# A decoder layer on one core: the first norm's steps put ahead of modulation rows and weight remainders, and a longer skew in the last down pass

## The chip, the cores and the metric

The kernel runs on one core of a Trainium2 chip. The time is what the device takes for one execution, in microseconds; the kernel before was run three times, and the median is 1267.68 us (1267.37 to 1270.29). Another execution was profiled, and the rows below are from it. The engines of the core are TensorE (PE: matmuls and transposes; PEld is its weight load), VectorE (DVE), ScalarE (ACT), GpSimd (POOL) and SyncE (SP), which here issues all transfers.

## The reference

The kernel computes one layer of a decoder over 256 tokens of width 2048, in float32. A conditioning vector gives six modulation vectors (shift, scale, gate for each of two sub-layers). The first sub-layer mixes tokens in two groups of heads and ends with an output projection; the second is a gated feed-forward network of inner width 5632. After each, a layer norm:

```python
mod = c_act @ w_mod[l] + b_mod[l]
sh1, sc1, g1, sh2, sc2, g2 = jnp.split(mod[:, None, :], N_MOD, axis=-1)
u = x * (1.0 + sc1) + sh1
y = token_mixer(u, w_in[l], conv_w[l], conv_b[l], b_igate[l], b_fgate[l],
                mlstm_norm_w[l], hgrn_norm_w[l], lb_all[l], w_out[l])
x = layer_norm(DEEPNORM_ALPHA * x + (1.0 + g1) * y, ln1_g[l], ln1_b[l])
u = x * (1.0 + sc2) + sh2
y = swiglu(u, w_gate[l], w_up[l], w_down[l])
x = layer_norm(DEEPNORM_ALPHA * x + (1.0 + g2) * y, ln2_g[l], ln2_b[l])
```

## The kernel before

**Weights in two parts.** Every float32 weight tile (128 x 1024, 512 KB) is loaded by SyncE into a buffer of `wr` (four of them), ScalarE copies it to the rounded type that TensorE takes (`wh`, five buffers), and VectorE subtracts that copy from the original: the remainder `wl` (five buffers). Activations are split likewise. A product is then three matmuls (`three`, L710 to L717): high x high (L713), low x high (L714), high x remainder (L717). `w1` (L699) makes one such tile.

**Modulation rows.** `mod(j)` (L171 to L174) loads one block of 128 rows of the modulation weight (1 MB) into one of two buffers of `mr` and reduces it on VectorE against the conditioning vector into a column of `modc`. There are 96: 32 at the start, 34 drawn by `mods_some` through the mixer and the output projection (`modq`), 14 named `late`, two of which `some(2)` issues for each k from 2 on in the first feed-forward groups, and 16 later. From these columns `affine1(c)` makes scale and shift for a quarter c of the normalised activations (`sc`, lines 786 to 788). The quarters 2 and 3 take them from `late` rows, quarter 3 from the last of them.

**Output projection** (L750 to L775). Two parts, four column groups c, four weight tiles each; the 256 tokens are two halves t, each with a PSUM bank. In the last group all four tiles are taken for half 0 and then for half 1. After each group `resid` scales the bank by the gate and adds it to z (L724, L728), and `stat` gathers the norm's statistics (L731).

**First norm.** `norm1(t)` aggregates (L735), takes logarithm and exponential on ScalarE, and scales z in four pieces (L802). `turn` transposes z on TensorE (L809, 16 transposes for a half) and `make_u2` applies scale and shift on ScalarE and splits the result into `u2h` and `u2l` (L830). A quarter c of u2 is used by the feed-forward blocks k = 4c to 4c + 3.

**Feed-forward.** The first two inner groups run together (`ffn_in((0, 1))`): 16 blocks k, each with two weight tiles and 24 matmuls, using all eight PSUM banks. k = 0 and 1 are done for half 0, then half 1 is transposed, then they are done for half 1. Nine more groups follow one by one, in two stretches, each with a pass of the down projection behind it (`down`); SiLU (`swi`) takes the banks at the end of a group. `fix` and `affine` (L914, L915) prepare z for the second residual on VectorE.

**The end.** The last down pass takes inner blocks 24 to 43, ten weight tiles for each of four column groups. In the last group the last `skew` = 8 blocks (four tiles) are done for half 0, then for half 1. Then `resid`, `stat` and `finish(t)`: the norm, two VectorE steps for each of four pieces (L970, L971), and the store.

**Order.** Each engine works through its instructions in an order fixed when the program is built. A planner lists the instructions as they become ready in its own estimate of time and takes the one earliest in the program first; `tc.high_priority(n)` lets instructions count as n places earlier in the program, and `add_manual_dep` with this kind of dependency sets only an order. Weight copies and remainders have n = 400.

Of the kernel before, what the change touches and what calls it, by code (L numbers as in the profile page):

```python
# [3 lines left out]
F32 = mybir.dt.float32  # L4
F32R = mybir.dt.float32r
U8 = mybir.dt.uint8
AF = mybir.ActivationFunctionType
ALU = mybir.AluOpType

P = 128  # L10
# [5 lines left out]
ALPHA = 2.0 ** 0.25  # L16
# [21 lines left out]
FIRST = 34  # L38
MIX = (("qk g i", "first"), ("v", "second"), ("o", "p last n"))
NATIVE = ((), ())  # L40
PRI = dict(w=400, e=0, m=-200)

PK = {}
_at = 0
# [10 lines left out]
RATE = (0.45, 0.4, 0.5)  # L55
# [24 lines left out]
def build(nc, tc, d):  # L80
    from contextlib import ExitStack

    with ExitStack() as ctx:
        cst = ctx.enter_context(tc.tile_pool(name="cst", bufs=1))
        wr = ctx.enter_context(tc.tile_pool(name="wr", bufs=CFG["wr"]))
        wh = ctx.enter_context(tc.tile_pool(name="wh", bufs=CFG["wh"]))
        wl = ctx.enter_context(tc.tile_pool(name="wl", bufs=CFG["wl"]))
# [6 lines left out]
        cnt = [0]  # L94
# [5 lines left out]
        def M(n=1024, name="m", dt=F32):  # L100
            cnt[0] += 1
            return med.tile([P, n], dt, tag="m", name=f"{name}{cnt[0]}")
# [11 lines left out]
        table = {"set": None, "load": None, "used": []}  # L114
# [19 lines left out]
        tt = nc.vector.tensor_tensor  # L134
# [36 lines left out]
        def mod(j):  # L171
            t = mr.tile([P, D], F32, tag="m", name=f"m{j}")
            nc.sync.dma_start(t, d["wmod"][j])
            table["mod"] = nc.vector.tensor_tensor_reduce(t, t, cb, 1.0, init[:, j : j + 1], ALU.mult, ALU.add, modc[:, j : j + 1]).ins  # L174
            yield

        def run(gen):
            for _ in gen:
                pass
# [440 lines left out]
        def mods_some(a):  # L620
            credit[0] += a
            while credit[0] >= 1:
                credit[0] -= 1
                next(modq, 0)
# [38 lines left out]
        for names, gen, n in PLAN:  # L663
# [4 lines left out]
            c = 0.0  # L668
# [27 lines left out]
                act(o[:, 512 * c : 512 * c + 512], bank, AF.Copy)  # L696
            return o

        def w1(src):  # L699
            cnt[0] += 1  # L700
            r = wr.tile([P, 1024], F32, tag="w", name=f"wr{cnt[0]}")
            nc.sync.dma_start(r, src)
            h = wh.tile([P, 1024], F32R, tag="h", name=f"wh{cnt[0]}")
            l = wl.tile([P, 1024], F32R, tag="l", name=f"wl{cnt[0]}")
            with tc.high_priority(PRI["w"]):
                act(h, r, AF.Copy)
                tt(l, r, h.bitcast(F32), ALU.subtract)  # L707
            return h, l

        def three(banks, h, l, a, b, first, last):  # L710
# [10 lines left out]
        def resid(t, c, bank, gate, scale):  # L721
            w = slice(512 * c, 512 * c + 512)
            m = S(512, "s5", bufs=CFG["s5"])
            tt(m, bank, gate[:, w], ALU.mult)  # L724
            if scale is None:
                tt(z[t][:, w], z[t][:, w], m, ALU.add)
            else:
                stt(z[t][:, w], z[t][:, w], scale, m, ALU.mult, ALU.add)  # L728

        def stat(t, c):  # L730
            nc.vector.bn_stats(st[t][:, 6 * c : 6 * c + 6], z[t][:, 512 * c : 512 * c + 512])  # L731
# [18 lines left out]
        for part in (1, 0):  # L750
            for c in range(4):
                if part:
                    banks[c] = [ps(), ps()]
                tiles = []
                skew = part == 0 and c == 3
                for p in range(4):
                    tiles.append(w1(d["wo"][16 * (1 - part) + 4 * c + p]))
                    mods_some(RATE[2])
                    if not skew:
                        for t in range(2):  # L760
                            for j in range(2):
                                k = 8 * part + 2 * p + j
                                w = slice(512 * j, 512 * j + 512)
                                three([banks[c][t]], tiles[-1][0][:, w], tiles[-1][1][:, w], half(yh, k, t), half(yl, k, t), part == 1 and k == 8, part == 0 and k == 7)
                if skew:
                    for t in range(2):
                        for p in range(4):
                            for j in range(2):
                                k = 2 * p + j
                                w = slice(512 * j, 512 * j + 512)  # L770
                                three([banks[c][t]], tiles[p][0][:, w], tiles[p][1][:, w], half(yh, k, t), half(yl, k, t), False, k == 7)
                if part == 0:
                    for t in range(2):
                        resid(t, c, banks[c][t], G1, ALPHA)
                        stat(t, c)  # L775
        run(modq)
        late = order2[FIRST:]

        def some(n):
            for _ in range(n):  # L780
                if late:
                    run(mod(late.pop(0)))

        def affine1(c):
            w = slice(4 * c, 4 * c + 4)
            tt(Ac[:, w], pc("l1g", 4 * c, 4), modc[:, 64 + 4 * c : 68 + 4 * c], ALU.mult)
            tt(Bc[:, w], pc("l1b", 4 * c, 4), modc[:, 64 + 4 * c : 68 + 4 * c], ALU.mult)
            tt(Bc[:, w], Bc[:, w], modc[:, 48 + 4 * c : 52 + 4 * c], ALU.add)

        affine1(0)  # L790
        affine1(1)
        u2h = [M(name="u2h", dt=F32R) for _ in range(4)]
        u2l = [M(name="u2l", dt=F32R) for _ in range(4)]

# [3 lines left out]
        def norm1(t):  # L798
            mu, rs = norm(t)
            for c in range(4):  # L800
                w = slice(512 * c, 512 * c + 512)
                ts(z[t][:, w], z[t][:, w], mu, rs, ALU.subtract, ALU.mult)  # L802

        zt = {}

        def turn(t, c):
            bank = ps()
            for j in range(4):
                nc.tensor.transpose(bank[:, P * j : P * j + P], z[t][:, 512 * c + P * j : 512 * c + P * j + P], ident)  # L809
            if c < 2:  # L810
                zt[t, c] = bank
                return
            if t == 0:
                zt[c] = M(name="zt")
            zt[t, c] = zt[c][:, 512 * t : 512 * t + 512]
            act(zt[t, c], bank, AF.Copy)

        def make_u2(t, c):
            u = S(512, "s5", bufs=CFG["s5"])
            for j in range(4):  # L820
                k = 4 * c + j
                w = slice(P * j, P * j + P)
                act(u[:, w], zt[t, c][:, w], AF.Identity, scale=Ac[:, k : k + 1], bias=Bc[:, k : k + 1])

            def part(x):
                return x[c].rearrange("p (k t) -> p k t", t=T)[:, :, t * P : t * P + P]

            u3 = u.rearrange("p (k t) -> p k t", t=P)
            act(part(u2h), u3, AF.Copy)
            tt(part(u2l), u3, part(u2h).bitcast(F32), ALU.subtract)  # L830
# [40 lines left out]

            return bk, held, block

        norm1(0)
        for c in range(4):
            turn(0, c)
            if c < 2:
                make_u2(0, c)
        norm1(1)
        use_set(AF.Silu)  # L880
        tc.add_manual_dep(table["load"], table["var"].name, order, reason="table")
        bk, held, block = ffn_in((0, 1))
        for k in range(2):
            for g in range(2):
                held[k, g] = w1(d["wf"][g * KT + k])
            block(k, 0)
        for c in range(4):
            turn(1, c)
            if c < 2:
                make_u2(1, c)  # L890
        for k in range(2):
            block(k, 1)
        for k in range(2, KT):
# [44 lines left out]
        def down(k0, k1, G, last):  # L938
            for c in range(4):
                bk = [ps(), ps()]  # L940
                held = {}
                skew = 8 if last and c == 3 else 0

                def pair(k, t):
                    for j in range(2):
                        w = slice(512 * j, 512 * j + 512)
                        three([bk[t]], held[k][0][:, w], held[k][1][:, w], hslice(k + j, t, 0), hslice(k + j, t, 1), k + j == k0, k + j == k1 - 1)

                for k in range(k0, k1, 2):
                    held[k] = w1(d["wd"][22 * c + k // 2])  # L950
                    if k < k1 - skew:
                        for t in range(2):
                            pair(k, t)
                    if k == k0 + 4:
                        while pend:
                            flip(pend.pop(0))
                for t in range(2):
                    for k in range(k1 - skew, k1, 2):
                        pair(k, t)
                    resid(t, c, bk[t], G, None)  # L960
                    if last:
                        stat(t, c)
                        if c == 3:
                            finish(t)

        def finish(t):
            mu, rs = norm(t)
            for c in range(4):
                w = slice(512 * c, 512 * c + 512)
                stt(z[t][:, w], z[t][:, w], mu, Lg[:, w], ALU.subtract, ALU.mult)  # L970
                stt(z[t][:, w], z[t][:, w], rs, Lb[:, w], ALU.mult, ALU.add)  # L971
                nc.sync.dma_start(d["out"][t][:, w], z[t][:, w])
# [73 lines left out]
```

## Time and profile before

| | |
|---|---|
| three runs | 1267.37, 1267.68, 1270.29 us |
| profiled execution | 1270.38 us, its span 1268.6 us |
| TensorE busy | 1216.6 us, 96% |
| VectorE busy | 900.4 us, 71% |
| ScalarE busy | 588.6 us, 46% |
| moved by DMA | 328 MB, 259 GB/s in the mean |

The span is the time from the first instruction to the last. An engine's line gives its busy time and share of the span. The chain that ended last is followed back from the last instruction to whatever released it, step by step. In rows in order of time the first number is the start and the second the time to the end of the last instruction in the row; the bracket at the end is how long the engine had been idle and what released it. Matmuls overlap: each lasts 0.39 us, and they start 0.2265 us apart at full clock.

### The profile page before, as it was taken

What the parts mean: (1) busy time and instruction counts of PE and PEld (TensorE: products, weight loads), DVE (VectorE), ACT (ScalarE), POOL (GpSimd) and SP (SyncE); (2) the same over time, 40 slices, a digit from 0 to 9 for tenths busy, and PEclk for the clock granted to TensorE, in tenths of its full rate; (3) what the DMA queues carried; (4) which work ended last, traced back from release to release, by engine and by line L of the source; (5) the groups of instructions that cost most, each with busy time, mean ns of one, the idle gap of its engine ahead of it and who ended that gap; (6) DMA issues with size and microseconds to landing.
All of it is one profiled execution on the core that took longest, in us unless ns stands there. A gap on an engine that the chain in (4) does not pass through costs nothing.

```text
span 1268.6 us, 17191 instructions
## 1 busy us (share of the span) xinstructions
PE 1216.6 (96%) x6738; PEld 1045.5 (82%) x6738; DVE 900.4 (71%) x979; ACT 588.6 (46%) x740; POOL 3.9 (0%) x13
## 2 busy tenths in 40 slices
PE   4899999899999999899999999999999999999995
PEld 4888899898889888688888888888888888888884
DVE  6778997999989979997876554455555445445655
ACT  4554454826665643654544444433434444434340
POOL 0000000000000000000000000000000000000000
PEclk9999999899999999899999999999999999999998
DMA  9998897857888989889998666566565666675551
GB/s 363 386 339 326 340 413 266 298 191 280 274 308 312 349 309 326 298 317 349 327 340 281 189 191 192 162 195 198 188 196 191 190 188 191 189 259 184 195 186 67
DMA packets 75969, 328.02 MB, mean 259 GB/s; under 512 B 8432, under 2 KB 8816, under 8 KB 62704
## 3 DMA queue, kind: packets, MB, share of 16 engines
q1 hardware_dynamic: 75888, 326.92, 73.5%
q8 instruction: 53, 0.87, 0.3%
q14 instruction: 28, 0.23, 0.1%
HBM read 324.79 MB, written 2.10 MB: 258 GB/s over the span
## 4 chain that ended last, share of the span: by engine, by line
PE 89%; DVE 6%; ACT 2%; issue 2%; DMA 1%; DVEq 0%; ACTq 0%
PE ps L713 21%; PE ps L714 21%; PE ps L717 21%; PE ps L249 5%; PE ps L251 5%; PE ps L250 5%; DVE m L174 2%; PE ps L260 2%; PE ps L261 2%; PE ps L262 2%; PE ps L445 1%; DVE wl L213 1%; ACT wh L128 1%; PE ps L855 1%; DMA m<-in_wmod 1%
## 5 line engine op out<-in xcount | busy, mean ns | idle before, releaser
L128 ACT ACTIVATE wh<-wr 128x1024 fp32r<-128x1024 f32 x408 | 431.1, 1059 | 554.5 <-PE ps L714 413.1
L707 DVE TENSOR_TENSOR wl<-wr,wh 128x1024 fp32r<-128x1024 f32 x296 | 360.7, 1224 | 291.0 <-ACT wh L128 287.8
L713 PE MATMUL ps<-wh,u2h 128*128 128x512 f32 x704 | 275.5, 392 | 0.0
L714 PE MATMUL ps<-wh,u2l 128*128 128x512 f32 x704 | 273.8, 389 | 0.0
L174 DVE CUSTOM_DVE_ANT_0 m<-m,cb,init 128x2048 f32<-128x2048 f32 x96 | 225.0, 2346 | 19.9 <-DMA m<-in_wmod 19.5
L717 PE MATMUL ps<-wl,u2h 128*128 128x512 f32 x704 | 217.2, 389 | 0.0
L249 PE MATMUL ps<-uh,wh 128*128 128x256 f32 x640 | 185.5, 294 | 22.3 <-ACT wh L128 17.2
L250 PE MATMUL ps<-ul,wh 128*128 128x256 f32 x640 | 182.4, 287 | 0.0
L251 PE MATMUL ps<-uh,wl 128*128 128x256 f32 x640 | 181.0, 288 | 1.1 <-DVE wl L213 1.0
L713 PEld LDWEIGHTS ps<-wh,u2h 128*128 128x128 f32 x704 | 132.6, 189 | 28.1 <-ACT u2h L128 0.7
L714 PEld LDWEIGHTS ps<-wh,u2l 128*128 128x128 f32 x704 | 132.3, 188 | 27.7 <-DVE u2l L830 0.4
L717 PEld LDWEIGHTS ps<-wl,u2h 128*128 128x128 f32 x704 | 132.2, 188 | 27.4
L213 DVE TENSOR_TENSOR wl<-wr,wh 128x1024 fp32r<-128x1024 f32 x112 | 135.6, 1221 | 25.4 <-ACT wh L128 24.8
L249 PEld LDWEIGHTS ps<-uh,wh 128*128 128x128 f32 x640 | 124.4, 196 | 25.0 <-ACT wh L128 17.8
L713 PE MATMUL ps<-wh,hid 128*128 128x512 f32 x352 | 137.2, 390 | 0.0
L717 PE MATMUL ps<-wl,hid 128*128 128x512 f32 x352 | 137.0, 389 | 0.0
L714 PE MATMUL ps<-wh,hid 128*128 128x512 f32 x352 | 137.0, 389 | 0.0
L250 PEld LDWEIGHTS ps<-ul,wh 128*128 128x128 f32 x640 | 125.4, 196 | 1.2 <-issue 1.0
L251 PEld LDWEIGHTS ps<-uh,wl 128*128 128x128 f32 x640 | 123.9, 196 | 1.9 <-DVE wl L213 1.8
L717 PEld LDWEIGHTS ps<-wl,hid 128*128 128x128 f32 x352 | 66.1, 188 | 13.8
L713 PEld LDWEIGHTS ps<-wh,hid 128*128 128x128 f32 x352 | 66.1, 188 | 13.7
L714 PEld LDWEIGHTS ps<-wh,hid 128*128 128x128 f32 x352 | 66.1, 188 | 13.5
(179 smaller groups left out, 1020.7 us busy)
## 6 DMA issues: line engine op xcount, KB each, us to landing
m<-in_wmod SPq DMA_DIRECT2D x96, 1024.0 KB, 7.0
wr<-in_wf SPq DMA_DIRECT2D x176, 512.0 KB, 3.7
wr<-in_win SPq DMA_DIRECT2D x112, 512.0 KB, 6.1
wr<-in_wd SPq DMA_DIRECT2D x88, 512.0 KB, 3.6
wr<-in_wo SPq DMA_DIRECT2D x32, 512.0 KB, 5.3
xT<-in_x SPq DMA_DIRECT2D x4, 512.0 KB, 7.7
z<-in_xr SPq DMA_DIRECT2D x2, 1024.0 KB, 8.5
out<-z SPq DMA_DIRECT2D x8, 256.0 KB, 2.4
```

Source lines behind the costliest of these rows:

```text
L128: i = nc.scalar.activation(out, in_, f, **kw).ins
L174: table["mod"] = nc.vector.tensor_tensor_reduce(t, t, cb, 1.0, init[:, j : j + 1], ALU.mult, ALU.add, modc[:, j : j + 1]).ins
L213: tt(l[:, :m], r[:, :m], h[:, :m].bitcast(F32), ALU.subtract)
L249: mm(o, h[:, wsl], kt(uh, k0 + k), start=st, stop=False, skip_group_check=True)
L250: mm(o, h[:, wsl], kt(ul, k0 + k), start=False, stop=False, skip_group_check=True)
L251: mm(o, l[:, wsl], kt(uh, k0 + k), start=False, stop=en, skip_group_check=True)
L260: mm(o, a, h[:, w], start=first and k == 0, stop=False, skip_group_check=True)
L261: mm(o, a, l[:, w], start=False, stop=False, skip_group_check=True)
L707: tt(l, r, h.bitcast(F32), ALU.subtract)
L713: mm(o, a, h[:, w], start=first, stop=False, skip_group_check=True)
L714: mm(o, b, h[:, w], start=False, stop=False, skip_group_check=True)
L717: mm(o, a, l[:, w], start=False, stop=last, skip_group_check=True)
```

## The change

The last group's residual steps, the first norm of both halves, the transposes and the first two quarters of u2 get a higher precedence (2500 for half 0, 2000 for half 1) than weight copies and remainders. The remainders of three of the first four feed-forward tiles are ordered behind the last scaling of half 0, and all `late` rows behind the last scaling of half 1. In the output projection's last group no rows are drawn. In the last down pass the skew is 14 blocks (seven tiles), and every second of these tiles takes its copy and remainder in two buffers of the pool `med` (`M`, ten buffers), which holds the u2 tiles before; there the residual steps of the last group get the precedence 2500.

```diff
-PRI = dict(w=400, e=0, m=-200)
+PRI = dict(w=400, e=0, m=-200, c=2500)
+SKEW = 14
...
-        def w1(src):
+        def w1(src, spare=False):
...
-            h = wh.tile([P, 1024], F32R, tag="h", name=f"wh{cnt[0]}")
-            l = wl.tile([P, 1024], F32R, tag="l", name=f"wl{cnt[0]}")
+            if spare:
+                h, l = M(name="mh", dt=F32R), M(name="ml", dt=F32R)
+            else:
+                h = wh.tile([P, 1024], F32R, tag="h", name=f"wh{cnt[0]}")
+                l = wl.tile([P, 1024], F32R, tag="l", name=f"wl{cnt[0]}")
             with tc.high_priority(PRI["w"]):
                 act(h, r, AF.Copy)
-                tt(l, r, h.bitcast(F32), ALU.subtract)
+                table["low"] = tt(l, r, h.bitcast(F32), ALU.subtract).ins
...
                 for p in range(4):
                     tiles.append(w1(d["wo"][16 * (1 - part) + 4 * c + p]))
-                    mods_some(RATE[2])
+                    if part or c < 3:
+                        mods_some(RATE[2])
...
                     for t in range(2):
-                        resid(t, c, banks[c][t], G1, ALPHA)
-                        stat(t, c)
+                        with tc.high_priority(PRI["c"] - 500 * t):
+                            resid(t, c, banks[c][t], G1, ALPHA)
+                            stat(t, c)
...
                     run(mod(late.pop(0)))
+                    after(table["mod"], normed[1])
...
-        affine1(0)
-        affine1(1)
+        with tc.high_priority(PRI["c"] + 500):
+            affine1(0)
+            affine1(1)
...
-                ts(z[t][:, w], z[t][:, w], mu, rs, ALU.subtract, ALU.mult)
+                table["norm"] = ts(z[t][:, w], z[t][:, w], mu, rs, ALU.subtract, ALU.mult).ins
+
+        def after(i, first):
+            tc.add_manual_dep(i, first.name, order, reason="late")
...
-        norm1(0)
-        for c in range(4):
-            turn(0, c)
-            if c < 2:
-                make_u2(0, c)
-        norm1(1)
+        with tc.high_priority(PRI["c"]):
+            norm1(0)
+            for c in range(4):
+                turn(0, c)
+                if c < 2:
+                    make_u2(0, c)
+        normed = [table["norm"]]
+        with tc.high_priority(PRI["c"] - 500):
+            norm1(1)
+        normed.append(table["norm"])
...
                 held[k, g] = w1(d["wf"][g * KT + k])
+                if k or g:
+                    after(table["low"], normed[0])
             block(k, 0)
-        for c in range(4):
-            turn(1, c)
-            if c < 2:
-                make_u2(1, c)
+        with tc.high_priority(PRI["c"] - 500):
+            for c in range(4):
+                turn(1, c)
+                if c < 2:
+                    make_u2(1, c)
...
-                skew = 8 if last and c == 3 else 0
+                skew = SKEW if last and c == 3 else 0
...
-                    held[k] = w1(d["wd"][22 * c + k // 2])
+                    held[k] = w1(d["wd"][22 * c + k // 2], k >= k1 - skew and (k - k1) % 4 == 0)
...
-                    resid(t, c, bk[t], G, None)
-                    if last:
-                        stat(t, c)
-                        if c == 3:
-                            finish(t)
+                    with tc.high_priority(PRI["c"] if last and c == 3 else 0):
+                        resid(t, c, bk[t], G, None)
+                        if last:
+                            stat(t, c)
+                    if last and c == 3:
+                        finish(t)
```

## Rows read from the trace of the kernel before

**Rows 1.** The page: the engines' busy time, and the chain that ended last by engine.

```profile
PE 1216.6 (96%) x6738; PEld 1045.5 (82%) x6738; DVE 900.4 (71%) x979; ACT 588.6 (46%) x740; POOL 3.9 (0%) x13
...
PE 89%; DVE 6%; ACT 2%; issue 2%; DMA 1%; DVEq 0%; ACTq 0%
```

**Rows 2.** Busy time by stretches: the stretch and its length, each engine's busy time and instructions, then TensorE's granted clock, the DMA engines' share and what they moved in GB/s.

```profile
515.00:520.00 5.00, 4.11 (x17) 3.78 (x18) 5.00 (x10) 3.18 (x11) 0.00 (x0) 0.50 1.01 415
520.00:540.00 20.00, 20.00 (x92) 15.92 (x91) 19.03 (x25) 16.12 (x33) 0.00 (x0) 0.97 0.70 248
540.00:560.00 20.00, 20.00 (x90) 16.58 (x89) 18.49 (x21) 9.62 (x10) 0.00 (x0) 1.00 0.95 346
590.00:600.00 10.00, 10.00 (x46) 8.29 (x45) 8.21 (x8) 3.56 (x4) 0.00 (x0) 1.00 1.00 365
```

**Rows 3.** VectorE in order of time around the first norm.

```profile
498.18 1.22 DVE L707 TENSOR_TENSOR wl<-wr,wh 128x1024 fp32r<-128x1024 f32 x1
...
504.64 0.67 DVE L724 TENSOR_TENSOR s<-ps,bc 128x512 f32<-128x512 f32 x1
505.23 2.34 DVE L174 CUSTOM_DVE_ANT_0 m<-m,cb,init 128x2048 f32<-128x2048 f32 x1
...
507.50 4.63 DVE L707 TENSOR_TENSOR wl<-wr,wh 128x1024 fp32r<-128x1024 f32 x4
512.04 0.68 DVE L728 SCALAR_TENSOR_TENSOR z<-z,s 128x512 f32<-128x512 f32 x1
...
514.44 0.25 DVE L735 BATCH_NORM_AGGREGATE mv<-st 128x2 f32<-128x24 f32 x1
...
515.29 1.92 DVE L802 TENSOR_SCALAR z<-z,mv 128x512 f32<-128x512 f32 x4
...
517.31 2.34 DVE L174 CUSTOM_DVE_ANT_0 m<-m,cb,init 128x2048 f32<-128x2048 f32 x1
```

**Rows 4.** TensorE in order of time there: the output projection's last matmul, the transposes of half 0, the first feed-forward matmuls, the transposes of half 1.

```profile
509.19 0.39 PE L717 MATMUL ps<-wl,yh 128*128 128x512 f32 x1
515.89 3.67 PE L809 MATMUL ps<-kc,z 128*128 128x128 f32 x16 [6.32 <-DVE z L802]
519.47 2.00 PE L713 MATMUL ps<-wh,u2h 128*128 128x512 f32 x4
...
525.86 1.91 PE L809 MATMUL ps<-kc,z 128*128 128x128 f32 x16
```

**Rows 5.** ScalarE in order of time there.

```profile
505.31 1.06 ACT L128 ACTIVATE wh<-wr 128x1024 fp32r<-128x1024 f32 x1 [5.74 <-DVE s L724]
...
514.73 0.29 ACT L128 ACTIVATE mv<-mv,eps 128x1 f32<-128x1 f32 x1 [4.28 <-DVE sc L786]
515.05 0.20 ACT L128 ACTIVATE mv<-mv 128x1 f32<-128x1 f32 x1
517.05 1.85 ACT L128 ACTIVATE s<-ps,sc 128x128 f32<-128x128 f32 x5 [1.79 <-PE ps L809]
518.77 0.65 ACT L128 ACTIVATE u2h<-s 128x512 fp32r<-128x512 f32 x1
```

**Rows 6.** VectorE in order of time: modulation rows. The first two are the ends of a run of ten; 445.42 is the 66th of all 96, the last before the `late` ones (505.23 and 517.31 above are the sixth and seventh of these), 563.52 the 80th, the last `late` one, and L788 behind it closes the last quarter's shift.

```profile
380.78 2.35 DVE L174 CUSTOM_DVE_ANT_0 m<-m,cb,init 128x2048 f32<-128x2048 f32 x1
...
424.17 2.35 DVE L174 CUSTOM_DVE_ANT_0 m<-m,cb,init 128x2048 f32<-128x2048 f32 x1 [1.21 <-DMA m<-in_wmod]
...
445.42 2.35 DVE L174 CUSTOM_DVE_ANT_0 m<-m,cb,init 128x2048 f32<-128x2048 f32 x1
...
563.52 2.34 DVE L174 CUSTOM_DVE_ANT_0 m<-m,cb,init 128x2048 f32<-128x2048 f32 x1
...
566.93 0.15 DVE L788 TENSOR_TENSOR sc<-sc,modc 128x4 f32<-128x4 f32 x1
```

**Rows 7.** SyncE's issues of transfers in order of time after the first norm.

```profile
508.75 3.73 SPq L702 DMA_DIRECT2D wr<-in_wf  x4
...
513.01 0.42 SPq L839 DMA_DIRECT2D bc<-in_l1b  x1
...
533.63 0.33 SPq L702 DMA_DIRECT2D wr<-in_wf  x1
```

**Rows 8.** ScalarE in order of time at the end of the first feed-forward groups: the first SiLU.

```profile
605.80 0.60 ACT L128 ACTIVATE s<-ps 128x512 f32<-128x512 f32 x1 [0.53 <-PE ps L717]
```

**Rows 9.** The instructions of the line that loads modulation rows, from 500 to 600 us: the time from issue to landing.

```profile
DMA to landing us min/median/max: 4.9/7.4/8.5
```

**Rows 10.** VectorE in order of time at the end.

```profile
1242.16 1.23 DVE L707 TENSOR_TENSOR wl<-wr,wh 128x1024 fp32r<-128x1024 f32 x1 [1.49 <-ACT wh L128]
1249.46 0.69 DVE L724 TENSOR_TENSOR s<-ps,bc 128x512 f32<-128x512 f32 x1 [6.07 <-PE ps L717]
...
1257.24 0.68 DVE L724 TENSOR_TENSOR s<-ps,bc 128x512 f32<-128x512 f32 x1
```

**Rows 11.** TensorE in order of time at the end: half 0's last matmul, and the first and last of half 1's 24 behind it.

```profile
1249.03 0.39 PE L717 MATMUL ps<-wl,hid 128*128 128x512 f32 x1
1249.26 0.39 PE L713 MATMUL ps<-wh,hid 128*128 128x512 f32 x1
...
1254.47 0.39 PE L717 MATMUL ps<-wl,hid 128*128 128x512 f32 x1
```

**Rows 12.** ScalarE in order of time at the end: the last weight copy.

```profile
1241.07 1.06 ACT L128 ACTIVATE wh<-wr 128x1024 fp32r<-128x1024 f32 x1 [1.66 <-PE ps L714]
```

## The prediction

> **What bounds the kernel now.** I read the page first [rows 1]: TensorE is busy 96% of the span and is 89% of the chain that ended last, so time is won only where TensorE stands idle or runs slowly, and lost wherever it is made to wait. Next the table by stretches [rows 2]: one place stands out. From 515 to 520 us TensorE is idle in part and runs at a granted clock of 0.50, which is the lower of its two levels, 1.2 GHz. Then the order of time of VectorE, TensorE and ScalarE there and at the end, where TensorE has no more work [rows 3 to 5, 10 to 12], and last what the change pushes out of the first place: the modulation rows [rows 6 to 9].
>
> At the first norm TensorE starts its last output-projection matmul at 509.19 us and its next work, the transposes, at 515.89 us, after 6.32 us idle [rows 4]. VectorE is why [rows 3]: it has half 0's first step (L724) at 504.64, but then takes a modulation row (2.34 us) and four weight remainders (4.63 us) before the next step (L728) at 512.04. In the tail VectorE works through half 0's normalisation until 1257.24 and only then takes half 1, whose matmuls began their last step at 1254.47 [rows 10, 11].
>
> **The first norm, gain.** The old cost is three terms: 6.32 us idle; 16 transposes that took 3.67 us at the low clock against 1.91 us later, 1.76 us; four matmuls in 2.00 us [rows 4], where three pitches of 0.2265 us and one matmul of 0.39 make 1.07 at full clock [rows 11], 0.93 us. Sum 9.0 us: the most there is to win. In the new order half 0 goes L724 at 504.64, two steps at a pitch of 0.60 us, the aggregate at 506.45 for 0.25 us; ScalarE is inside a weight copy until 506.37 and then needs 0.52 us for the logarithm and exponential (514.73 to 515.25) [rows 3, 5], so z is scaled from 507.25 to 509.2, before the output projection ends at 509.58. If the transposes stand after it, the first u2 piece comes 0.7 us (four transposes) and 2.37 us (ScalarE, 517.05 to 519.42) later [rows 5], at 512.65: gain 519.47 + 0.93 - 512.65 = 7.7 us. If they are laid among the last matmuls, the wait vanishes: 9.0 us. I take 8.3. Bounds: 9.0 above; nothing below, should TensorE reach the transposes before z is scaled. The three weight remainders put behind the last scaling (3.4 us of VectorE, done by about 514) are wanted from 513.6 on, one each 1.36 us, and the first is done by 510.4, so they cost 0; uncovered they would cost 1.15 us each. Half 1's chain is hidden by 5.4 us of half-0 matmuls. In the earlier column groups the precedence delays a remainder by at most three steps, 1.8 us; the output projection's last remainder ended at 499.4 [rows 3] and is needed 30 matmuls before 509.4, at 502.6, so I cost it at 0, at most 1.8. Leaving out `mods_some` in the last group changes nothing: the first 34 rows that it draws from end with the one at 445.42 [rows 6].
>
> **The first norm, price.** All fourteen `late` rows must now follow half 1's last scaling. Before, six of them ran after 445.42 and up to 505.23, beside output-projection matmuls; eight ran from 517.31 to 563.52 [rows 3, 6]. The last ends at 565.87 and lets the modulation column L788 be made at 566.93, from which u2's last quarter follows. TensorE wants that quarter at k = 12. ScalarE's first SiLU at 605.80 waited for the first half-block of k = 15; so k = 15 began 1.36 us earlier, and k = 12 three blocks of 24 matmuls at 0.2265 us earlier, at 588.1 [rows 8, 11]: the old slack is some 20 us. After the change k = 12 would be reached at 588.1 - 8.3 = 579.8.
>
> When do fourteen rows end? Two are loaded beforehand (the pool has two buffers), at 515.5 and 517.9 by my order. The third load can be issued only when the first row's buffer is read, so twelve periods follow. Bounds for one period: 4.82 us, the mean of nine intervals from 380.78 to 424.17, and 6.60 us, the mean of seven from 517.31 to 563.52 in this very stage [rows 3, 6]. The nearest row is the transfer rate: with the DMA engines at a share of 1.00 they moved 365 GB/s [rows 2]; weights at TensorE's pace take 0.524 MB per 2.72 us, 193 GB/s; the 172 GB/s left carry a 1.049 MB row in 6.1 us. I take 6.1 for eight periods, 5.0 for the first two (before, no weight was issued from 512.5 to 533.6 [rows 7], since the buffers were full) and 4.8 for the last two, when TensorE stands and weights stop: 10 + 48.8 + 9.6 = 68.4. The last row starts at 517.9 + 68.4 = 586.3, ends at 588.7; L788 and ScalarE's 2.37 us bring TensorE back at 591.3. That is a wait of 11.5 us, and k = 12 comes 3.2 us later than before instead of 8.3 earlier. After that idle time I charge the same slow restart as the old one, 1.76 + 0.93 = 2.7 us. First norm in sum: 5.9 us lost. With 4.82 the twelve take 57.8, TensorE is back at 580.7, waits 0.9 and 7.4 are won; with 6.60 it is back at 602.1, 14.0 + 2.7 = 16.7 lost. Rows queue on SyncE with the weights: a row issue that waits for a buffer holds back weight issues behind it, which is how the stage could go to the upper figure.
>
> The Trainium skill, HBM Reference, section Specifications, bears on this: it gives about 358 GB/s as a core's share and about 425 GB/s for a core that streams alone. This trace shows 365 GB/s at a full share of weights and rows, and 415 GB/s only while broadcast loads ran [rows 2, 7]. By 425 a row would take 4.5 us and the wait would vanish (rival one); by 358 it would take 6.4.
>
> **The tail.** Skewing 14 weight rows instead of 8 puts seven weight tiles instead of four in the half-0-then-half-1 order. Half 1 then has 18 more matmuls behind half 0's last: 18 x 0.2265 = 4.08 us. Half 0's last begins at 1249.03 - 4.08 = 1244.95, and L724, 0.43 us behind it as before, at 1245.38. Its chain of 7.78 us (1249.46 to 1257.24) ends at 1253.16. Half 1's L724 can start 0.43 us behind 1254.47, at 1254.90, instead of at 1257.24: 2.34 us won; what follows is the same [rows 10, 11]. The matmuls are as many. Seven held tiles don't fit five buffers; three go into buffers that have had no reader since the last projection. The half-0 pass starts at 1235.6 and uses a tile each 1.36 us, the last at 1243.8; even at the old cadence its copy was at 1241.07 and its remainder done at 1243.39 [rows 10, 12], so supply costs 0; uncovered, one tile late costs at most a period of 2.72 us less 1.36. Should half 1's first steps be set between half 0's last ones, up to two of these (0.67 us each) follow: bounds 1.0 to 2.34, I take 2.3.
>
> **Sum.** The profiled execution took 1270.38 us (span 1268.6 and 1.8 around it), 2.7 above the median of 1267.68. 1270.38 + 5.9 - 2.3 = 1274.0; against the median 1267.68 + 3.6 = **1271.3 us**.
>
> **Rivals.** *One: the rows come in time.* At 4.82 us a period both gains stand: 1267.68 - 7.4 - 2.3 = 1258.0. For it: landing takes as little as 4.9 us [rows 9], which with 2.35 us on VectorE and two buffers would allow even 3.6. Against it: the share of 0.95 from 540 to 560 us with six fewer rows [rows 2], when a full share is 1.00. The 425 GB/s of the Trainium skill's HBM Reference would speak for it. *Two, the slower side: the rows keep their old period of 6.60 us*, since they share two in-order queues with the weights; TensorE waits for u2's last quarter until 602.1: 1267.68 + 16.7 - 2.3 = 1282.1. It turns slower than before as soon as the period passes about 5.4 us: with TensorE back at 587.7 the 2.3 of the tail pay for the restart. For it: it is this stage's own mean; against it: DMA share was only 0.70 from 520 to 540 us, so part of that mean was not transfer. *Three: the first norm doesn't move*, because TensorE meets transposes set too early and waits there, while rows stay in time: only the tail remains, 1265.4.
>
> **Chances.** The forecast 0.42, with its own range 1267 to 1276 (period 5.6 to 6.3 for the middle eight); rival one 0.30; rival two 0.16; rival three 0.12. A measurement can tell 0.3%, 3.8 us, from no change: below 1263.9 is faster, above 1271.5 slower. Half of the forecast lies on either side of the upper mark: faster 0.30 (rival one), same 0.21 + 0.12 = 0.33, slower 0.21 + 0.16 = 0.37. The range, 1257.5 to 1280, leaves out half of rival two and the edge of rival one.
>
> **What would show it.** In the new profile: VectorE's L724, L728, L731 and aggregate of half 0 without anything between them; transposes by 510; no row between 450 and 514, then fourteen; TensorE idle before k = 12 with ScalarE's u2 copies as releaser and behind them a row; a granted clock near half after it; in the tail half 1's L724 within 0.5 us of the last matmul. The prediction is wrong if the last of the fourteen rows ends before 577 (rival one), or if TensorE waits for weights in that stage as well.

## The result, and the profile after

The changed kernel takes **1277.44 us** (median of 4 runs, 1276.14 to 1278.14), the kernel before 1268.29 beside it: a ratio of 1.0067 [1.0055, 1.0079], slower by some 9 us. The forecast was 1271.3, with a range of 1267 to 1276 for its own account and of 1257.5 to 1280 over all. The profiled execution took 1277.67 us with a span of 1275.8, 7.2 more than before. Three executions beside the experiments came out far slower than all others (1377.81 and 2479.51 us of the kernel before, 6940.89 of e2) and are left out of every median and ratio.

The page of the changed kernel, busy time and the chain that ended last. TensorE's busy time stands beside rows 1.

```profile
PE 1222.0 (96%) x6738; PEld 1046.7 (82%) x6738; DVE 903.2 (71%) x979; ACT 588.1 (46%) x740; POOL 3.9 (0%) x13
PE 86%; DVE 6%; DMA 4%; ACT 2%; issue 2%; DVEq 0%; SPq 0%; ACTq 0%
```

TensorE's share of the chain fell from 89% to 86% and transfers now hold 4% of it. Where, the table by stretches of the changed kernel tells (TensorE, its weight loads, VectorE, ScalarE, GpSimd busy with counts; granted clock, DMA share, GB/s):

```profile
515.00:520.00 5.00, 5.00 (x21) 4.04 (x20) 5.00 (x9) 2.54 (x5) 0.00 (x0) 0.69 0.37 116
520.00:540.00 20.00, 20.00 (x93) 16.46 (x92) 18.37 (x19) 11.90 (x19) 0.00 (x0) 1.00 0.83 278
540.00:560.00 20.00, 18.42 (x80) 14.58 (x79) 19.08 (x22) 7.54 (x13) 0.00 (x0) 1.00 0.82 303
560.00:570.00 10.00, 5.86 (x12) 3.67 (x12) 10.00 (x13) 1.21 (x2) 0.00 (x0) 0.66 0.97 362
570.00:580.00 10.00, 6.19 (x24) 4.27 (x24) 9.79 (x13) 3.02 (x3) 0.00 (x0) 0.98 1.00 391
580.00:600.00 20.00, 19.95 (x82) 16.42 (x83) 14.11 (x14) 14.44 (x20) 0.00 (x0) 0.93 0.82 284
```

and of the kernel before, the later stretches that stand in no group:

```profile
560.00:570.00 10.00, 10.00 (x45) 8.27 (x45) 10.00 (x14) 5.41 (x9) 0.00 (x0) 1.00 0.73 243
570.00:580.00 10.00, 10.00 (x46) 8.27 (x45) 9.60 (x11) 6.33 (x10) 0.00 (x0) 1.00 0.92 333
580.00:600.00 20.00, 20.00 (x90) 16.58 (x89) 14.65 (x14) 7.80 (x8) 0.00 (x0) 1.00 0.95 351
```

From 515 to 520 us TensorE no longer stands [rows 2]. But from 560 to 580 it ran 36 matmuls instead of 91: at 0.2265 us each [rows 11] that is 12.5 us; ten fewer from 540 to 560 and eight fewer from 580 to 600 (90 each before) add 4.1. What it waited for, in order of time on TensorE of the changed kernel:

```profile
562.97 0.80 PE L717 MATMUL ps<-wh,u2h 128*128 128x512 f32 x1 [4.00 <-ACT wh L129]
570.96 0.51 PE L717 MATMUL ps<-wh,u2h 128*128 128x512 f32 x1 [2.03 <-ACT wh L129]
580.05 0.80 PE L717 MATMUL ps<-wh,u2h 128*128 128x512 f32 x1 [2.74 <-ACT wh L129]
```

Three times it is a weight tile's copy. ScalarE's copies, in order of time, show what they waited for in turn, and the last row when the first SiLU came (605.80 before [rows 8]):

```profile
561.87 1.06 ACT L129 ACTIVATE wh<-wr 128x1024 fp32r<-128x1024 f32 x1 [7.06 <-DMA wr<-in_wf]
569.85 1.06 ACT L129 ACTIVATE wh<-wr 128x1024 fp32r<-128x1024 f32 x1 [6.93 <-DMA wr<-in_wf]
578.94 1.06 ACT L129 ACTIVATE wh<-wr 128x1024 fp32r<-128x1024 f32 x1 [6.77 <-DMA wr<-in_wf]
...
615.53 0.60 ACT L129 ACTIVATE s<-ps 128x512 f32<-128x512 f32 x1 [0.52 <-PE ps L721]
```

The loads themselves were late. SyncE's queue in that time alternates two rows (L174) with one or two weight tiles (L703), and sends eleven tiles as soon as the rows are through:

```profile
552.22 3.80 SPq L174 DMA_DIRECT2D m<-in_wmod  x2
556.12 0.39 SPq L703 DMA_DIRECT2D wr<-in_wf  x1
560.50 3.20 SPq L174 DMA_DIRECT2D m<-in_wmod  x2
563.80 0.86 SPq L703 DMA_DIRECT2D wr<-in_wf  x2
568.59 3.20 SPq L174 DMA_DIRECT2D m<-in_wmod  x2
571.89 20.53 SPq L703 DMA_DIRECT2D wr<-in_wf  x11
```

From 552 to 572 us six rows but three weight tiles were issued, where TensorE uses a tile per 2.72 us, seven in that time. SyncE's row issues waited for VectorE to free one of the two row buffers, 43.8 us in sum from 515 to 572.

VectorE in order of time: the norm's chain of half 0, the second and the last of the fourteen rows, and the tail.

```profile
502.20 0.69 DVE L728 TENSOR_TENSOR s<-ps,bc 128x512 f32<-128x512 f32 x1 [1.23 <-PE ps L721]
502.93 0.69 DVE L732 SCALAR_TENSOR_TENSOR z<-z,s 128x512 f32<-128x512 f32 x1
503.65 0.69 DVE L735 BATCH_NORM_STATS2 st<-z 128x6 f32<-128x512 f32 x1
504.38 0.27 DVE L739 BATCH_NORM_AGGREGATE mv<-st 128x2 f32<-128x24 f32 x1
506.05 1.92 DVE L810 TENSOR_SCALAR z<-z,mv 128x512 f32<-128x512 f32 x4 [1.41 <-ACT mv L129]
...
522.69 2.35 DVE L175 CUSTOM_DVE_ANT_0 m<-m,cb,init 128x2048 f32<-128x2048 f32 x1
...
577.59 2.35 DVE L175 CUSTOM_DVE_ANT_0 m<-m,cb,init 128x2048 f32<-128x2048 f32 x1
...
1255.10 0.69 DVE L728 TENSOR_TENSOR s<-ps,bc 128x512 f32<-128x512 f32 x1 [8.62 <-PE ps L721]
...
1264.62 0.69 DVE L728 TENSOR_TENSOR s<-ps,bc 128x512 f32<-128x512 f32 x1 [1.65 <-PE ps L721]
```

No row and no weight remainder stands in the chain any more (512.04 was its second step before [rows 3]). But VectorE waits 1.41 us in it for ScalarE, where a weight copy stands between the logarithm and the exponential:

```profile
504.68 0.30 ACT L129 ACTIVATE mv<-mv,eps 128x1 f32<-128x1 f32 x1 [0.28 <-DVE mv L739]
504.88 1.04 ACT L129 ACTIVATE wh<-wr 128x1024 fp32r<-128x1024 f32 x1
505.83 0.19 ACT L129 ACTIVATE mv<-mv 128x1 f32<-128x1 f32 x1
```

TensorE's rows there, half 0's last matmul of the projection, the transposes (L820), the last projection matmul and the first one behind the norm:

```profile
501.77 0.39 PE L721 MATMUL ps<-wl,yh 128*128 128x512 f32 x1
...
506.65 2.02 PE L820 MATMUL ps<-kc,z 128*128 128x128 f32 x16
...
509.23 0.40 PE L721 MATMUL ps<-wl,yh 128*128 128x512 f32 x1
512.80 1.19 PE L717 MATMUL ps<-wh,u2h 128*128 128x512 f32 x4 [3.17 <-ACT u2h L129]
```

In the kernel before, half 0's last matmul of the projection was this one:

```profile
503.75 0.39 PE L717 MATMUL ps<-wl,yh 128*128 128x512 f32 x1
```

The account against the profiled execution before, from these rows: half 0's last bank was ready 1.98 us earlier (501.77 for 503.75); the first norm gave 4.69 more (0.46 of it because VectorE, still at the group before, took that bank only at 504.64 [rows 3]), so that the feed-forward began 6.67 earlier (512.80 for 519.47 [rows 4]); from there to the first SiLU it took 16.40 longer, which leaves 9.73 lost; the tail gave 2.35 back (its last step stands 7.38 later, 1264.62 for 1257.24 [rows 10]).

### The profile page after: what moved, and what is told of

Its sections match the earlier page's. It is cut to its first block, busy times and chain, and to the rows that moved or that the text cites. A ratio compares the mean times of both kernels' runs of the same rounds, so it can differ in the third digit from the quotient of the medians.

```text
span 1275.8 us, 17183 instructions
## 1 busy us (share of the span) xinstructions
PE 1222.0 (96%) x6738; PEld 1046.7 (82%) x6738; DVE 903.2 (71%) x979; ACT 588.1 (46%) x740; POOL 3.9 (0%) x13
## 4 chain that ended last, share of the span: by engine, by line
PE 86%; DVE 6%; DMA 4%; ACT 2%; issue 2%; DVEq 0%; SPq 0%; ACTq 0%
PE ps L718 20%; PE ps L721 20%; PE ps L717 20%; PE ps L250 5%; PE ps L252 5%; PE ps L251 5%; DVE m L175 3%; DMA m<-in_wmod 2%; PE ps L261 2%; PE ps L262 2%; PE ps L263 2%; PE ps L446 1%; DMA wr<-in_wf 1%; DVE wl L214 1%; ACT wh L129 1%
## 5 line engine op out<-in xcount | busy, mean ns | idle before, releaser
L717 PE MATMUL ps<-wh,hid 128*128 128x512 f32 x340 | 132.5, 390 | 0.0
L721 PE MATMUL ps<-wl,hid 128*128 128x512 f32 x340 | 132.3, 389 | 0.0
L718 PE MATMUL ps<-wh,hid 128*128 128x512 f32 x340 | 132.3, 389 | 0.0
L717 PEld LDWEIGHTS ps<-wh,hid 128*128 128x128 f32 x340 | 63.8, 188 | 13.2
L718 PEld LDWEIGHTS ps<-wh,hid 128*128 128x128 f32 x340 | 63.8, 188 | 13.1
```

The lines of the kernel that those rows point to most:

```text
L717: mm(o, a, h[:, w], start=first, stop=False, skip_group_check=True)
L718: mm(o, b, h[:, w], start=False, stop=False, skip_group_check=True)
L721: mm(o, a, l[:, w], start=False, stop=last, skip_group_check=True)
```

## The experiments

Two theories stood against each other. *Transfer*: the fourteen rows, held back, don't fit beside the weights into the stage that must take them, whoever waits in the end. *Order*: they would fit, but their issues, each waiting for a row buffer on SyncE, hold up the weights behind them. Each median stands against the kernel before, run beside it (medians of 1268.16, 1269.11 and 1268.85). Diffs are against the changed kernel where nothing else is said.

**The hold taken out (e1).**

```diff
                     run(mod(late.pop(0)))
-                    after(table["mod"], normed[1])
```

> The changed kernel, but the late rows may run whenever they are loaded; everything else of the change stays. If the price is the fourteen rows pushed into the feed-forward stage, their transfers leave that stage, TensorE's waits between 556 and 582 us (9.5 us, plus the slow restarts) go, and the chain's own gain appears: 1257 to 1261 us. If the price is the precedence itself (transposes laid among the output projection's last matmuls, three remainders held, other work put behind), it stays: 1270 us or more.

Measured 1263.94 (1261.68 to 1264.85), ratio 0.9960 [0.9946, 0.9975]: 13.5 us less than with the hold. The hold is the whole of the loss and more. It missed the lower times expected, because precedence alone doesn't keep rows out of the chain; VectorE in order of time:

```profile
502.17 0.69 DVE L728 TENSOR_TENSOR s<-ps,bc 128x512 f32<-128x512 f32 x1 [0.15 <-PE ps L721]
502.78 2.34 DVE L175 CUSTOM_DVE_ANT_0 m<-m,cb,init 128x2048 f32<-128x2048 f32 x1
...
505.04 0.69 DVE L732 SCALAR_TENSOR_TENSOR z<-z,s 128x512 f32<-128x512 f32 x1
...
506.46 2.35 DVE L175 CUSTOM_DVE_ANT_0 m<-m,cb,init 128x2048 f32<-128x2048 f32 x1
...
509.59 1.92 DVE L809 TENSOR_SCALAR z<-z,mv 128x512 f32<-128x512 f32 x4
```

Two rows still stand between the chain's steps, z is scaled at 509.59 instead of 506.05, and TensorE waits 3.52 us for it.

**The hold alone (e2), against the kernel before.**

```diff
                     run(mod(late.pop(0)))
+                tc.add_manual_dep(table["mod"], normed[1].name, order, reason="late")
```

> The kernel before, with only the late rows ordered behind half 1's last scaling; no precedence, old tail. If the held rows are the price, it is slower than before by what they cost, 10 to 20 us, so 1278 to 1288 us, and TensorE again waits for weights whose transfers are late. If the precedence is the price, it stays within 3 us of the kernel before.

Measured 1277.18 (three runs, 1276.78 to 1279.22), ratio 1.0068 [1.0043, 1.0093], just under the 1278 to 1288 expected. Added to the kernel before and without the tail, the hold costs some 9 us, net of what it frees of VectorE for the norm. No trace of these runs was kept, so that TensorE waits for weights here too is not shown.

**The tail alone (e3), against the kernel before.**

```diff
-                skew = 8 if last and c == 3 else 0
+                skew = SKEW if last and c == 3 else 0
...
-                    held[k] = w1(d["wd"][22 * c + k // 2])
+                    held[k] = w1(d["wd"][22 * c + k // 2], k >= k1 - skew and (k - k1) % 4 == 0)
...
+                    with tc.high_priority(PRI["c"] if last and c == 3 else 0):
```

> The kernel before with only the tail's edits: skew 14, three weight tiles in spare buffers, the last residual steps first. By the sum 2.3 us faster than before, 1266.0 us against 1268.3; the rival that half 1's first steps come between half 0's last ones gives 1267.3.

Measured 1267.07 (10 runs), ratio 0.9976 [0.9961, 0.9992], 3.0 us; the forecast's 2.3 lies inside. VectorE's two L728 are as far apart as in the changed kernel, 1253.72 - 1244.20 = 9.52 us, 42 matmuls at 0.2265.

**The late rows issued on GpSimd's queue (e4).**

```diff
-                    run(mod(late.pop(0)))
+                    run(mod(late.pop(0), nc.gpsimd))
```

> The changed kernel, with the late rows' loads issued from GpSimd's queue instead of SyncE's, still held behind half 1's last scaling. If weight loads were late because they stood behind row loads in SyncE's order, weights now go out as their buffers come free and TensorE's waits for weights nearly vanish; what may be left is a wait for u2's last quarter at k = 12: 1262 to 1270 us. If the transfer rate itself is what is short, the rows take the same share of it and the time stays at 1274 us or more.

Measured 1280.71, ratio 1.0091 [1.0072, 1.0110]. The order theory falls: weights were issued without a row before them, TensorE waited for none, and the time is no better. TensorE, and VectorE's second and last late row:

```profile
522.80 2.35 DVE L175 CUSTOM_DVE_ANT_0 m<-m,cb,init 128x2048 f32<-128x2048 f32 x1
...
590.36 2.35 DVE L175 CUSTOM_DVE_ANT_0 m<-m,cb,init 128x2048 f32<-128x2048 f32 x1 [0.38 <-DMA m<-in_wmod]
597.71 1.22 PE L717 MATMUL ps<-wh,u2h 128*128 128x512 f32 x2 [14.95 <-ACT u2h L129]
```

The rows now take (590.36 - 522.80) / 12 = 5.63 us each, and TensorE waits 14.95 us for u2's last quarter. Here is the prediction's own wait. In these two runs the queue's order decides who waits, not how long. Each row load on GpSimd's queue still waited for VectorE to free one of the two row buffers; what a third buffer would do was not tried. From issue to landing a row took 7.3 us in the median there, for 5.9 on SyncE's queue in the changed kernel (both from 505 to 600), so that the choice of GpSimd's queue itself can have a part in the 5.63; no other queue was tried.

**The row halved: reduced by half (e10), loaded by half (e6), both (e11).** e10 loads the whole row and reduces its left half; e6 loads the left half and reduces it twice; e11 loads and reduces the left half once.

```diff
+            nc.sync.dma_start(t[:, 0:1024], d["wmod"][j][:, 0:1024])
+            t = t[:, 0:1024]
+            table["mod"] = nc.vector.tensor_tensor_reduce(t, t, cb[:, 0:1024], 1.0, init[:, j : j + 1], ALU.mult, ALU.add, modc[:, j : j + 1]).ins
```

> The changed kernel with all fourteen late rows held, but each loads only the left half of its row (0.5 MB) and reduces that half twice, so VectorE works as long as before while the transfers are halved (the result leaves out the right halves). If transfer is what the stage lacks, TensorE's waits between 550 and 585 us vanish: 1256 to 1262 us. If VectorE's time or the order of its queue is what it lacks, the time stays at 1273 us or more.

> The changed kernel, all fourteen rows held, each loaded in full, but only the left half reduced (the result leaves out the right halves): the transfers as in the changed kernel, VectorE's work for these rows halved, 17 us less between 518 and 585 us. If VectorE's time is what the stage lacks, the waits mostly go: 1258 to 1266 us. If it is the transfer, or the order in which rows and weights are issued, 1272 us or more.

> As the run with the half reduction, but only the left half is loaded too: both demands halved. If either demand alone was short in turn (transfer in the changed kernel, VectorE with the half loads), 1256 to 1262 us. If it is still 1272 us or more, neither amount but the order of the queues with only two row buffers sets the price.

e6 measured 1280.54, ratio 1.0088 [1.0074, 1.0102]; e10 1274.72, 1.0045 [1.0030, 1.0060]; e11 1264.65, 0.9959 [0.9944, 0.9974]. e6 upsets the theory that transfer alone is short: with half the rows' bytes nothing was won. A third theory, that VectorE is short as well, is what e10 and e11 were for. One stretch of e6, TensorE's wait there, and the same stretch of e11:

```profile
540.00:560.00 20.00, 20.00 (x90) 16.53 (x89) 19.50 (x29) 11.51 (x18) 0.00 (x0) 1.00 0.85 287
599.42 1.22 PE L726 MATMUL ps<-wh,u2h 128*128 128x512 f32 x2 [17.30 <-ACT u2h L129]
```

```profile
540.00:560.00 20.00, 20.00 (x90) 16.58 (x89) 19.38 (x30) 10.50 (x16) 0.00 (x0) 1.00 0.91 313
560.00:580.00 20.00, 20.00 (x90) 16.57 (x89) 16.45 (x22) 12.71 (x19) 0.00 (x0) 1.00 0.84 280
```

In e6 VectorE is 19.50 of 20 us busy while the DMA share is 0.85, and the wait is for u2's last quarter, 17.30 us. In e10 VectorE is freed, and TensorE still waits 9.0 us in sum for weights. Halving either gives little or nothing, halving both cures the stage (no wait for weights or for that quarter in e11).

An estimate from rows of these traces agrees. In the 62 us from 520 to 582 TensorE at full pace uses 23 weight tiles. With the twelve rows not loaded beforehand that is 24.6 MB, 397 GB/s, where 376 GB/s moved from 560 to 580 in the changed kernel. VectorE needs 14 x 2.35 us for rows and 23 x 1.16 for remainders (4.63 for four [rows 3]), 60 of the 62, before u2's remainders. So VectorE and the transfers are both near their end there. Of VectorE's busy time in the changed kernel, 9.5 us in this stretch are steps that only prepare the second residual (L932, L933); what holding those back would give was not tried.

How much of e6 is VectorE's own time and how much its order isn't told apart: its VectorE has 2.4 us of 20 free from 560 to 580, and the two reductions of a row don't stand together in it. The twelfth row's first ran at 577.83 and its second at 584.53; the next row's first, which waited 1.93 us for its load, and two remainders stand between. So the last row's load, which needs that buffer, was issued at 585.85 only.

**Ten held instead of fourteen (e5), ten held to half 0's scaling (e7), nine (e8).**

```diff
+                    held = len(late) <= 10
                     run(mod(late.pop(0)))
-                    after(table["mod"], normed[1])
+                    if held:
+                        after(table["mod"], normed[1])
```

> The changed kernel, holding back only the last ten of the fourteen late rows; the first four may run beside the output projection again. If the price grows with the bytes pushed into the feed-forward stage, four rows fewer (4.2 MB, 11 to 12 us of transfer at 365 to 378 GB/s) leave no wait for weights or u2, and the chain is as clean as in the changed kernel: 1257 to 1261 us, 2 to 4 us faster than with all rows free. If any hold costs, it lies between 1264 and 1277.

> As the run that holds the last ten rows, but only behind half 0's last scaling, about 11 us earlier. If half 1's chain has room (it is hidden by half 0's matmuls), the same time within 2 us, 1257 to 1262 us; if rows then get between half 1's steps and TensorE has to wait for its transposes, some 2 to 5 us slower than that run.

> As the run that holds the last ten rows, but nine. The fifth row runs before the chain in any case, so within 1.5 us of that run; if the transfers of the feed-forward stage were still the limit there, 2 us faster.

e5 measured 1263.04 (1257 to 1261 was expected), ratio 0.9953 [0.9940, 0.9966]; e7 1263.84, 0.9954 [0.9942, 0.9966]; e8 1262.24, 0.9946 [0.9932, 0.9959]: all alike, and 14 us better than fourteen held. Four rows fewer after the norm suffice: in e5 the last row starts at 562.66 us, 15 earlier, and the only wait for a weight left in the stage is 0.68 us. Against e1, which holds none, they gain at most 1.8 us by the ratios, inside the intervals: that holding ten beats holding none is not shown. What remains is a wait before the feed-forward; TensorE of e5:

```profile
511.72 2.02 PE L717 MATMUL ps<-wh,u2h 128*128 128x512 f32 x4 [3.18 <-ACT u2h L129]
```

and ScalarE's queue ahead of it:

```profile
508.34 1.06 ACT L129 ACTIVATE wh<-wr 128x1024 fp32r<-128x1024 f32 x1 [2.31 <-PE ps L718]
509.31 1.84 ACT L129 ACTIVATE s<-ps,sc 128x128 f32<-128x128 f32 x5
511.02 0.65 ACT L129 ACTIVATE u2h<-s 128x512 fp32r<-128x512 f32 x1
```

A weight copy waits 2.31 us for TensorE to free its buffer, and u2's first piece stands behind it in order.

**u2's first piece ahead of that copy (e9), on e5.** The weight copies of k = 1 are ordered behind half 0's exponential, those of k = 2 behind u2's first copy.

```diff
                 held[k, g] = w1(d["wf"][g * KT + k])
+                if k:
+                    after(table["high"], var0)
...
+                if k == 2:
+                    after(table["high"], first_u2)
```

> The run that holds the last ten rows, with two more orders on ScalarE: the weight copies of k = 1 behind half 0's exponential, and those of k = 2 behind the first u2 copy. In the changed kernel ScalarE stood 2.3 us in a copy that waited for TensorE (509.43) while the first transposes had been done since 507.2. If that order is what TensorE's 3.18 us before the first feed-forward matmul come from, the wait falls below 1 us and the slow restart behind it goes too: 3 to 5 us faster than that run, 1258 to 1260 us. If u2 itself is the limit, within 1 us of it.

Measured **1261.28** (1260.35 to 1263.48), ratio 0.9939 [0.9924, 0.9954], the lowest median of all and faster than both kernels. Its interval overlaps e5's, and it missed the 1258 to 1260 expected. TensorE of e9:

```profile
512.31 1.19 PE L717 MATMUL ps<-wh,u2h 128*128 128x512 f32 x4 [1.79 <-ACT u2h L129]
514.41 0.73 PE L718 MATMUL ps<-wh,u2l 128*128 128x512 f32 x2 [0.91 <-DVE u2l L843]
```

The wait fell from 3.18 to 1.79 us, not below 1: another copy, at 508.94, still stood ahead. From half 0's first step on VectorE to the first feed-forward matmul it took 9.32 us (502.99 to 512.31) for 10.61 in e5 (501.11 to 511.72). But from 500 to 620 us TensorE's waits sum to 4.6 us for 3.9 in e5, since others came behind (0.91 for u2's remainder, 1.1 and 0.8 for weights), and the profiled execution was no faster than e5's. A gain over e5 is not shown.

## Why the prediction came out as it did

**Which side.** That the rows pushed behind the norm cost more than the norm gives held, as did the places: a clean chain, transposes before 510, no row in it, TensorE waiting in the feed-forward with a lower clock behind the wait.

**The norm's gain: too high.** 8.3 us was forecast, 4.69 came by the first feed-forward matmul. The chain was free of rows and remainders, and the transposes went among the last projection matmuls, the forecast's better case. But TensorE waited 3.17 us for u2's first piece and restarted slowly (a granted clock of 0.69 from 515 to 520). The step that failed is the end of the sum, where that piece was to come 2.37 us behind the transposes with ScalarE free: of the weights' work the forecast costed VectorE's remainders, and one copy on ScalarE that ends at 506.37, but not the copies behind it in ScalarE's in-order queue. In the changed kernel, as in e5, a copy (at 509.43) waited 2.31 us for a buffer ahead of u2; e9 removed part of that wait. Another (at 504.88) held the exponential, so that z was scaled 3.85 us behind the chain's first step (506.05 - 502.20), where the forecast had 2.61 (507.25 - 504.64). Of the 6.67 us by which the feed-forward began earlier, 1.98 came from earlier in the kernel. TensorE was busy 8.78 of the 10 us from 360 to 370 in the profiled execution before, and all 10 in the changed one; e3, which leaves this part as it was, has no such idle time either, so 1.22 of the 1.98 belongs to the execution and not to the edit. The rest is near a wait of 0.9 us for VectorE around 420 that the kernel before has, e3 too (0.8), and the changed kernel not; which edit takes it away was not tried.

**The rows' price: right in kind, mis-sized, and paid by another wait.** The forecast gave the weights their 193 GB/s first and the rows the rest, 6.1 us a row. On this side that share-out is the step that failed. In the run the rows went first: their period was (577.59 - 522.69) / 12 = 4.58 us, the last ended at 579.9 instead of 588.7, and u2's last quarter held nothing up. The weights went short instead. That is one of the two signs which the prediction named against itself, weights waited for in that stage. Rival one asked for 4.82 us a period and got better, yet its gain didn't come, since it took the weights' supply for granted. Only with a queue of their own (e4) did the rows wait as the forecast had it: 14.95 us for 11.5. The forecast's net for the first norm was 5.9 us lost; measured at the first SiLU it is 9.73, though 1.22 us came free with the execution. Two terms were short: a gain of 8.3 that gave 4.69, and a bill that counted bytes only. Fourteen rows at 2.35 us also take 33 us of a VectorE that is 18 to 19 of 20 us busy there [rows 2 and the table above], and e6 shows that halving the bytes alone doesn't pay it.

The transfer rate itself was near: 365 GB/s assumed, 362 and 391 measured where the share was 0.97 and 1.00; e4 moved 404 from 560 to 570, the most of any trace in the eight stretches of 10 us from 520 to 600. By the Trainium skill, HBM Reference, section Specifications, a core that streams alone may have about 425 GB/s; no trace of this stage reached it.

**The tail: right.** 2.34 us was forecast from the full shift and 2.35 measured, with half 1's step now waiting 1.65 us for TensorE instead of TensorE's result waiting for VectorE. The three tiles in spare buffers cost nothing: TensorE has no wait there from 1190 us on.

**The sum.** 1271.3 fell 6.1 us short of 1277.44: 3.8 in the first norm (9.73 for 5.9), and most of the rest because the profiled execution before, against which 9.73 is measured, stood 2.7 us above the median that the sum was set against, while the one after stands 0.2 above its own. The time lies outside the forecast's own range of 1267 to 1276. That it lies inside 1257.5 to 1280 is in part luck: this range reached up for rival two, rows at their old period of 6.60 us, and they came at 4.58.

## What to carry to other kernels

Before work is pushed behind a critical chain, add up its bytes and its engine time in the stage that must take it, for every engine and queue there, and ask who goes short when they don't fit; here a change of queue only moved the wait. Hold back no more than that stage can take: the same change won 5 to 7 us with no, nine or ten rows held and lost 9 with fourteen. And look, on each engine of the chain, at what stands ahead in its order waiting for a buffer; a short copy can hold the step that everything waits for.

## What the runs showed beyond that

The DMA engines at a share of 1.00 moved 391 GB/s from 570 to 580 us of the changed kernel and 365 before [rows 2]: a full share isn't one rate. After 4.00 us of idle time, TensorE's matmuls from 562.97 to 567.87 went at the lower clock (0.66 in that stretch); after 2.03 us more of idle time, from 570.96, they went at the full one (0.98).
